# A decoder trunk's opening: modulation sums in four chunks of 256 columns, the first on TensorE

## The chip, the cores and the metric

The kernel runs on one core of a Trainium2 chip. The metric is the device time of one execution in microseconds. A profiled execution leaves a trace from which the rows below are read. Engines: TensorE (PE in the rows; PEld are its weight loads), VectorE (DVE), ScalarE (ACT), GpSimd (POOL) and SyncE (SP), which issues most of the DMA transfers. Each engine works through its own queue in a fixed order.

## What is computed

A trunk of two layers for one sequence of 256 tokens of width 1024, all in float32. Each layer is a feed-forward block, a mixer (attention in the first layer, a gated recurrence in the second) and another feed-forward block. Each block sees a normed x, scaled and shifted by modulations that come from a vector c. Only the first block matters here:

```python
cond = jax.nn.silu(c)
mod = (cond @ ada_w[i] + ada_b[i]).reshape(B, N_SUB, 3, 1, D)   # shift, scale, gate
h = rms_norm(x, norm_g[i, 0]) * (1.0 + mod[:, 0, 1]) + mod[:, 0, 0]
x = x + 0.5 * mod[:, 0, 2] * swiglu(h, ffn_w_up[i, 0], ffn_w_down[i, 0])
```

D is 1024, the feed-forward width 2816. `ada_w[i]` has 1024 rows and 9 x 1024 columns, `ffn_w_up` 1024 rows and 2 x 2816 columns.

## The kernel before

**Products.** Activations lie with their features on the partitions: `hbuf[k]` holds feature block k (128 of 1024) for all 256 tokens. Float32 products are made of three products of rounded halves (`mm3`, lines 728 to 730): high weight by high h, high weight by low h, low weight by high h. So each weight is split after it is loaded: ScalarE casts it to the rounded type (`wh`), VectorE takes the difference (`wl`). In the opening these are lines 360 and 361, later 371 and 372. Likewise h has a high half (line 588, ScalarE) and a low half (line 589, VectorE).

**Loads.** `plan` writes one list of items in the order in which they are loaded, `emit_raw` issues their transfers on the sync queue into a ring of eight raw buffers of 512 KB, `take_raw` hands them out in order. An item is split by `split_gen`, one step at a time. `pump` calls such a step at each tick, a tick being the three matmuls of one `mm3`, as long as it is no more than two weight items ahead (`SPLIT_AHEAD`).

**Side tasks.** `side` starts a generator that yields how many ticks it wants to wait; `tick` goes on with those that are due and `drain` finishes those that are named. A planner then fixes the order of each engine's queue: by program order, but past an instruction that by its own clock is not ready yet. `issue_after(i)` holds an instruction behind i on its engine.

**The opening** (`setup`). x is loaded, its squares are summed on ScalarE (556), the reciprocal root is taken on GpSimd (558), x is transposed on PE (614) and copied by ScalarE (616). VectorE scales x by the root (561) and the result is transposed and copied again, giving `xn`. Meanwhile the shift and scale columns of the first block come in eight chunks of 128 columns ("adc" items, 1 MB each), each followed by one "upk" item: the 128 rows of `ffn_w_up` that answer to it, for the first seven column blocks (`HEAD = 7`, 2 x 7 x 128 columns, 0.9 MB). In `ada_chunk` VectorE multiplies each of the 8 row blocks of an adc item by its value of `cond` and adds up, in two chains (434, 436); `NPE = 0` means that none of them is summed from raw weights on PE. `head_mods` lets PE add over the partitions, with the running sum as the stationary side and a column of ones (448); VectorE adds the bias and makes the scale (454, 457). Then ScalarE shifts and scales one feature block (585) and both halves of h are made (588, 589).

The loop over q in `setup` issues, for each chunk, first its modulations and its h, and then the products of the chunk before it (`cur`, `head_products`: 14 groups of three matmuls, 42). The seven column blocks are all open in PSUM at once, so the 336 matmuls of the opening can follow the order in which the weights come. Then `ffn` goes on with the column blocks from 7 on.

## Time and profile before

| | us |
|---|---|
| median of 3 runs | 1105.64 |
| lowest, highest | 1105.61, 1108.42 |
| the profiled execution | 1107.98 |
| its span | 1106.1 |
| PE busy in it | 1084.1 |
| VectorE, ScalarE busy | 838.7, 587.9 |
| transferred | 260.24 MB, 235 GB/s over the span |

The profiled execution is a fourth one; the rows are from it alone. In rows of the timeline the first number is the start in us from the beginning of the span, the second the time in us until the last instruction of the row has ended. The end of a matmul is modelled and matmuls overlap, so the distance of their starts tells more than their length. In brackets stands the idle time of the engine ahead of the row and what ended it.

### The profile page before, as it was taken

To read this page: it belongs to the slowest core of one execution; us is meant where nothing else is said; L and a number is where in the kernel's file an instruction comes from. 1 tells how busy PE (TensorE), PEld (TensorE's weight loads), DVE (VectorE), ACT (ScalarE), POOL (GpSimd) and SP (SyncE) were. 2 spreads that over 40 slices of the span, in tenths; PEclk is the share of its full clock that TensorE was granted. 3 is DMA by queue.
4 is the path that set the end of the run, shared out by engine and by line. 5 is a ranking of instruction groups with operands and counts; after the bars stand their busy time and mean duration, and the time that the engine had idled before them with its cause. 6 is when DMAs were issued, how large, how long until landed. Compare 5 with 4: busy or idle time off the path is not lost.

```text
span 1106.1 us, 22061 instructions
## 1 busy us (share of the span) xinstructions
PE 1084.1 (98%) x8835; PEld 1055.6 (95%) x8835; DVE 838.7 (76%) x1486; ACT 587.9 (53%) x1105; POOL 23.1 (2%) x46
## 2 busy tenths in 40 slices
PE   6999999999999999999999999999999999999997
PEld 6999999988999999999999999999998999999997
DVE  6987789587996797888579888777987879555542
ACT  5454444376865664444355444445777756444443
POOL 0000000020000000000000000000000000000000
PEclk9999999999999999999999999999999999999999
DMA  9999998759974579998958999995643456665530
GB/s 300 334 316 316 323 330 266 213 168 328 298 236 137 162 221 313 312 320 307 259 173 252 286 335 320 322 294 172 191 145 117 122 157 190 188 189 173 179 109 39
DMA packets 304707, 260.24 MB, mean 235 GB/s; under 512 B 9525, under 2 KB 281501, under 8 KB 304605
## 3 DMA queue, kind: packets, MB, share of 16 engines
q1 hardware_dynamic: 304172, 257.79, 76.0%
q8 instruction: 69, 1.13, 0.4%
q0 software_dynamic: 288, 0.52, 0.2%
q10 hardware_dynamic: 144, 0.52, 0.1%
q14 instruction: 34, 0.27, 0.1%
HBM read 257.75 MB, written 1.05 MB: 234 GB/s over the span
## 4 chain that ended last, share of the span: by engine, by line
PE 76%; issue 18%; ACT 3%; POOL 1%; DMA 1%; DVE 1%; SPq 0%; POOLq 0%; DVEq 0%; ACTq 0%
PE pf L729 17%; PE pf L728 16%; PE pf L730 16%; PE pd L728 6%; PE pd L729 6%; PE pd L730 6%; PE pA L1172 1%; ACT wh L371 1%; PE pv L881 1%; PE pv L879 1%; PE pv L880 1%; PE adaps L465 1%; PE sc L998 1%; DMA raw<-in_ffn_w_up_dram 1%; PE pt L1020 1%
## 5 line engine op out<-in xcount | busy, mean ns | idle before, releaser
L729 PE MATMUL pf<-hbuf,wh 128*128 128x256 f32 (+1 forms) x1920 | 543.8, 284 | 0.9 <-DVE hbuf L589 0.9
L730 PE MATMUL pf<-hbuf,wl 128*128 128x256 f32 (+1 forms) x1920 | 543.2, 284 | 0.0
L728 PE MATMUL pf<-hbuf,wh 128*128 128x256 f32 (+1 forms) x1920 | 539.0, 284 | 0.6 <-ACT hbuf L588 0.6
L371 ACT CAST wh<-raw 128x1024 fp32r<-128x1024 f32 x338 | 341.6, 1027 | 370.1 <-PE pf L729 219.0
L372 DVE TENSOR_TENSOR wl<-raw,wh 128x1024 fp32r<-128x1024 f32 x338 | 400.2, 1194 | 158.3 <-ACT wh L371 157.1
L728 PEld LDWEIGHTS pf<-hbuf,wh 128*128 128x128 f32 x1920 | 363.4, 191 | 4.8 <-issue 4.0
L729 PEld LDWEIGHTS pf<-hbuf,wh 128*128 128x128 f32 x1920 | 365.1, 190 | 1.2 <-DVE hbuf L589 1.1
L730 PEld LDWEIGHTS pf<-hbuf,wl 128*128 128x128 f32 x1920 | 364.6, 190 | 0.8 <-issue 0.8
L728 PE MATMUL pd<-gx,wh 128*128 128x256 f32 x704 | 197.5, 281 | 0.0
L729 PE MATMUL pd<-gx,wh 128*128 128x256 f32 x704 | 196.7, 279 | 0.0
L730 PE MATMUL pd<-gx,wl 128*128 128x256 f32 x704 | 196.4, 279 | 0.0
L412 DVE SCALAR_TENSOR_TENSOR adaacc<-raw,cond,adaacc 128x1024 f32<-128x1024 f32 x112 | 142.9, 1276 | 0.9 <-DMA raw<-in_ada_w_dram 0.4
L728 PEld LDWEIGHTS pd<-gx,wh 128*128 128x128 f32 x704 | 132.3, 188 | 2.5 <-issue 2.5
L730 PEld LDWEIGHTS pd<-gx,wl 128*128 128x128 f32 x704 | 132.3, 188 | 0.0
L729 PEld LDWEIGHTS pd<-gx,wh 128*128 128x128 f32 x704 | 132.3, 188 | 0.0
L794 ACT CAST gx<-g 128x256 fp32r<-128x256 f32 x88 | 35.6, 406 | 25.8 <-DVE g L836 18.3
L796 DVE TENSOR_TENSOR gx<-g,gx 128x256 fp32r<-128x256 f32 x88 | 36.6, 418 | 0.2
L410 DVE TENSOR_SCALAR adaacc<-raw,cond 128x1024 f32<-128x1024 f32 x16 | 12.1, 756 | 25.4 <-PE adaps L465 25.4
L836 DVE TENSOR_TENSOR g<-sa,pf 128x256 f32<-128x256 f32 x73 | 30.1, 414 | 0.4 <-ACT sa L835 0.2
L801 DVE SCALAR_TENSOR_TENSOR x<-pd,mod,x 128x256 f32<-128x256 f32 x32 | 14.3, 479 | 20.5 <-PE pd L730 20.5
L835 ACT ACTIVATE sa<-pf 128x256 f32<-128x256 f32 x73 | 27.4, 377 | 0.0
L360 ACT CAST wh<-raw 128x896 fp32r<-128x896 f32 x16 | 15.0, 935 | 23.0 <-DMA raw<-in_ffn_w_up_dram 23.0
(218 smaller groups left out, 859.2 us busy)
## 6 DMA issues: line engine op xcount, KB each, us to landing
raw<-in_ffn_w_up_dram SPq DMA_DIRECT2D x162, 512.0 KB, 5.5
raw<-in_ada_w_dram SPq DMA_DIRECT2D x128, 512.0 KB, 5.8
raw<-in_ffn_w_down_dram SPq DMA_DIRECT2D x76, 512.0 KB, 5.7
raw<-in_fox_w_in_dram SPq DMA_DIRECT2D x32, 512.0 KB, 5.3
raw<-in_hgrn_w_in_dram SPq DMA_DIRECT2D x32, 512.0 KB, 4.5
raw<-in_ada_w_dram SPq DMA_DIRECT2D x32, 256.0 KB, 6.9
raw<-in_ffn_w_up_dram SPq DMA_DIRECT2D x16, 448.0 KB, 6.6
raw<-in_fox_w_out_dram SPq DMA_DIRECT2D x8, 512.0 KB, 5.1
```

What stands on the lines that cost most here:

```text
L360: nc.scalar.copy(wh[:, k, cs], raw)
L371: nc.scalar.copy(wh[:, ks, cs], raw)
L372: nc.vector.tensor_tensor(wl[:, ks, cs], raw, wh[:, ks, cs].bitcast(F32), ALU.subtract)
L412: nc.vector.scalar_tensor_tensor(self.ada_acc, raw, self.cond[:, k:k + 1], self.ada_acc, ALU.mult, ALU.add)
L728: nc.tensor.matmul(ps, wh, hx[:, :n], start=first, stop=False, skip_group_check=True)
L729: nc.tensor.matmul(ps, wh, hx[:, lo:lo + n], start=False, stop=False, skip_group_check=True)
L730: nc.tensor.matmul(ps, wl, hx[:, :n], start=False, stop=last, skip_group_check=True)
L794: nc.scalar.copy(dst[:, :S], v)
L796: nc.vector.tensor_tensor(dst[:, lo:lo + S], v, dst[:, :S].bitcast(F32), ALU.subtract)
L801: nc.vector.scalar_tensor_tensor(self.x[:, m, :], ps, gate[:, m:m + 1], self.x[:, m, :], ALU.mult, ALU.add)
L835: nc.scalar.activation(sa, ps[0], AF.Silu)
L836: nc.vector.tensor_tensor(g, sa, ps[1], ALU.mult)
```

## The change

The chunks are twice as wide (`QA = 256`), so that there are four adc items of 2 MB, each followed by two upk items (`HEAD_ORDER`). The first adc item is not touched by VectorE: PE multiplies the raw weights, as the stationary side, by the columns of `cond`, 8 row blocks by 4 column groups, and adds up in PSUM. The other three are summed by VectorE in one chain of 512 elements, and then by PE over the partitions in four matmuls. What follows the sums is a side task (`head_task`) with lags of 4 ticks and 1 tick; the products of a feature block follow its own h. The bias and scale of a chunk are two VectorE instructions.

x is scaled on ScalarE by pairs of feature blocks, in place of VectorE, and the first copies of x are shared between ScalarE and VectorE. Four of the weight casts' instructions (second half of the first upk item, first half of the second, high and low) are held behind the latest shift. Six small loads go to GpSimd's queue. The transposes of the small rows share a bank.

The diff without the import and some of the removed lines, which the functions above show:

```diff
@@ -36,9 +36,9 @@
 FOLD = (5, 4)
 H_LAG = 0
 HEAD = 7
-QW = 128
-NPE = 0
-DEEP = 3
+QA = 256
+HEAD_LAG = (4, 1)
+HEAD_ORDER = [(0, 2), (2, 2), (4, 2), (6, 2)]
 HG_LAG = (4, 3, 4, 10, 12)
 FOX_LAG = (24, 6)
 HG_ORDER = [("hgq", 0), ("hgv", 0), ("hgq", 1), ("hgq", 2), ("hgv", 1), ("hgq", 3),
@@ -208,8 +208,8 @@
             extra = []
             if pos == 0:
                 assert kind == "ffn"
-                for q in range(D // QW):
-                    items += [("adc", (l, s, q)), ("upk", (f, q))]
+                for q, (k0, nk) in enumerate(HEAD_ORDER):
+                    items += [("adc", (l, s, q))] + [("upk", (f, k)) for k in range(k0, k0 + nk)]
                 extra = ada(n, (2,))
             take = quota.get(n, 0) if len(subs) == 6 else 24
             must = 0
@@ -253,12 +253,11 @@
             l, s, q = p
             c0 = s * 3 * D
             w = r(a["ada_w"][l])[:, :, c0:c0 + 2 * D].rearrange("p k (u f) -> p k u f", u=2)
-            return [(None, w[:, :, :, q * QW:(q + 1) * QW])], (KC, 2 * QW)
+            return [(None, w[:, :, :, q * QA:(q + 1) * QA])], (KC, 2 * QA)
         if kind == "upk":
             f, q = p
             w = r(a["ffn_w_up"][f // 2, f % 2]).rearrange("p k (u f) -> p k u f", u=2)
-            n = QW // P
-            return [(None, w[:, q * n:(q + 1) * n, :, 0:HEAD * P])], (n, 2 * HEAD * P)
+            return [(None, w[:, q:q + 1, :, 0:HEAD * P])], (1, 2 * HEAD * P)
         if kind == "up":
             f, j = p
             w = r(a["ffn_w_up"][f // 2, f % 2])
@@ -347,19 +346,15 @@
             self.ready[i] = (kind, wh, wl)
             return
         if kind == "upk":
-            wh, wl = [self.wp.tile([P, 2048], F32R, tag=t, name=f"{t}{i}")[:, :2 * HEAD * QW]
...
+            wh, wl = [self.wp.tile([P, 2048], F32R, tag=t, name=f"{t}{i}")[:, :2 * HEAD * P] for t in ("wh", "wl")]
+            for u in range(2):
+                cs = slice(u * HEAD * P, (u + 1) * HEAD * P)
+                raw = self.take_raw()
+                with self.tc.issue_after(self.last_shift[0]) if p[1] + u == 1 else nullcontext():
+                    nc.scalar.copy(wh[:, cs], raw)
+                with self.tc.issue_after(self.last_shift[1]) if p[1] + u == 1 else nullcontext():
+                    nc.vector.tensor_tensor(wl[:, cs], raw, wh[:, cs].bitcast(F32), ALU.subtract)
+                yield
             self.ready[i] = (kind, wh, wl)
             return
         t = self.wp.tile([P, 2048], F32R, tag="wh", name=f"wh{i}")
@@ -416,45 +411,58 @@
     def ada_chunk(self, p):
         nc = self.nc
         l, s, q = p
-        n = QW // P
...
+        n = 1024 // (2 * QA)
+        if q == 0:
+            ps = self.bank("adac")
+            for c in range(KC // n):
+                raw = self.take_raw()
+                for i in range(n):
+                    k = n * c + i
+                    for o in range(2 * QA // P):
+                        nc.tensor.matmul(ps[:, o:o + 1], raw[:, i, o * P:(o + 1) * P], self.cond[:, k:k + 1],
+                                         start=(k == 0 and o == 0), stop=(k == KC - 1), skip_group_check=True)
+                yield
+            self.side(("head", q), self.head_task(q, ps, self.xn), True)
+            return
+        ac = self.wk.tile([P, 2 * QA], F32, tag="mx", name=f"adc{q}", bufs=6)
+        for c in range(KC // n):
             raw = self.take_raw()
-            for i in range(m):
...
+            for i in range(n):
+                k = n * c + i
+                if k == 0:
+                    nc.vector.tensor_scalar(ac, raw[:, i, :], self.cond[:, k:k + 1], None, ALU.mult)
                 else:
-                    v = nc.vector.scalar_tensor_tensor(ac[:, k % 2], raw[:, i, :], self.cond[:, k:k + 1],
-                                                       ac[:, k % 2], ALU.mult, ALU.add)
+                    nc.vector.scalar_tensor_tensor(ac, raw[:, i, :], self.cond[:, k:k + 1], ac, ALU.mult, ALU.add)
             yield
-        self.head_acc[q] = (ac, ps)
...
+        self.side(("head", q), self.head_task(q, ac, self.xn), True)
+
+    def head_task(self, q, ac, xn):
+        nc = self.nc
+        l, s = divmod(self.subs[0], NSUB)
+        n = QA // P
+        if q == 0:
+            ps = ac
+        else:
+            ps = self.bank("adac")
             for o in range(2 * n):
-                nc.tensor.matmul(ps[:, o:o + 1], ac[:, j, o * P:(o + 1) * P], self.ones[:, 0:1],
...
+                nc.tensor.matmul(ps[:, o:o + 1], ac[:, o * P:(o + 1) * P], self.ones[:, 0:1],
+                                 start=(o == 0), stop=True, skip_group_check=True)
+        yield HEAD_LAG[0]
+        b = l * 72 + s * 24 + q * n
+        m = self.head_mod[:, :, q * n:(q + 1) * n]
+        nc.vector.tensor_tensor(m, ps[:, :2 * n].rearrange("p (u j) -> p u j", u=2),
+                                pick(self.adab[:, b:], [8, 2], [1, n]), ALU.add)
+        g = (l * 3 + s) * 8 + q * n
+        nc.vector.scalar_tensor_tensor(m[:, 1], m[:, 1], 1.0, self.vec[:, g:g + n], ALU.add, ALU.mult)
+        yield HEAD_LAG[1]
+        for k in range(q * n, (q + 1) * n):
+            u = self.w("u")
+            nc.scalar.activation(u, xn[:, k, :], AF.Identity, scale=self.head_mod[:, 1, k:k + 1],
+                                 bias=self.head_mod[:, 0, k:k + 1])
+            h = self.hbuf[0][:, k, :]
+            v0 = nc.scalar.copy(h[:, :S], u)
+            v1 = nc.vector.tensor_tensor(h[:, HS:HS + S], u, h[:, :S].bitcast(F32), ALU.subtract)
+            self.last_shift = (v0.ins, v1.ins)
 
     def ada_finish(self, l, s, part, total):
         nc = self.nc
@@ -521,12 +529,10 @@
                  (cst, a["consts"][:, P:])]
         for dst, src in small[:2]:
             nc.sync.dma_start(dst, src)
-        small = small[2:]
+        for dst, src in small[2:]:
+            nc.gpsimd.dma_start(dst, src)
         while len(self.raw_queue) < RAW_BUFS:
             self.emit_raw()
-            for dst, src in small[:2]:
-                nc.sync.dma_start(dst, src)
-            small = small[2:]
         self.ones = cp.tile([P, P], F32, name="ones")
         nc.vector.memset(self.ones, 1.0)
         self.sel4 = cst[:, 128:132]
@@ -550,50 +556,40 @@
         self.sq = None
         self.fold = None
         self.closing = False
-        self.head_acc = {}
+        self.xn = xn
         ms = self.wk.tile([P, 2], F32, tag="rstd", name="rstd")
         for t in range(2):
             nc.scalar.activation(xs[t], xt[t], AF.Square, accum_out=ms[:, t:t + 1])
         nc.vector.tensor_scalar(ms, ms, 1.0 / D, EPS, ALU.mult, ALU.add)
         self.last_pow = nc.gpsimd.tensor_tensor(ms, ms, self.mhalf, ALU.pow).ins
-        self.load_x(xt, self.x)
-        for t in range(2):
-            nc.vector.tensor_scalar(xs[t], xt[t], ms[:, t:t + 1], None, ALU.mult)
+        self.load_x(xt, self.x, engines=(nc.scalar.copy, nc.vector.tensor_copy))
+        self.split_step()
+        self.split_step()
+        self.vec = cp.tile([P, 80], F32, name="vec")
+        self.adab = cp.tile([P, 144], F32, name="adab")
+        self.head_mod = cp.tile([P, 2, KC], F32, name="headmod")
         pr = self.bank("pr")
-        nc.tensor.transpose(pr[:, :80], rows, self.ident[:80, :80])
-        self.vec = cp.tile([P, 80], F32, name="vec")
+        nc.tensor.transpose(pr[:, 0:80], rows, self.ident[:80, :80])
+        for l in range(2):
+            nc.tensor.transpose(pr[:, P + l * 72:P + (l + 1) * 72], abr[:, l, :], self.ident[:72, :72])
         nc.vector.tensor_copy(self.vec, pr[:, :80])
-        pa = self.bank("pa")
...
+        nc.vector.tensor_copy(self.adab, pr[:, P:P + 144])
+        for k in range(0, KC, 2):
+            for t in range(2):
+                c = slice(k * P, (k + 2) * P)
+                nc.scalar.activation(xs[t][:, c], xt[t][:, c], AF.Copy, scale=ms[:, t:t + 1])
+            self.load_x(xs, xn, k, k + 2)
+            if k in (0, 4):
+                self.split_step()
         self.pf = [self.acc("pf") for _ in range(3)] + [self.bank("pf") for _ in range(HEAD - 3)]
         self.pf = [self.halves(p) for p in self.pf]
-        l, s = divmod(self.subs[0], NSUB)
...
+        while self.n_split < 1:
+            self.split_step()
+        self.drain({("head", 0)})
+        for k in range(KC):
             wh, wl = self.weights("upk")
-            cur = [(q * n + i, wh[:, i], wl[:, i]) for i in range(n)]
-        for t in cur:
-            self.head_products(*t)
+            self.drain({("head", k * P // QA)})
+            self.head_products(k, wh, wl)
         with self.tc.issue_after(self.last_pow):
             for o in (0, 64):
                 nc.gpsimd.memset(self.bf[o:o + 64, :], 0.0)
@@ -606,14 +602,15 @@
             nc.vector.tensor_copy(self.identb, self.ident)
             nc.vector.tensor_copy(self.maskb, cst[:, 0:P])
 
-    def load_x(self, src, dst):
-        nc = self.nc
-        for k in range(0, KC, 2):
+    def load_x(self, src, dst, k0=0, k1=KC, engines=None):
+        nc = self.nc
+        engines = engines or (nc.scalar.copy,)
+        for k in range(k0, k1, 2):
             px = self.bank("px")
             for i in range(4):
                 nc.tensor.transpose(px[:, i * P:(i + 1) * P], src[i % 2][:, (k + i // 2) * P:(k + i // 2 + 1) * P],
                                     self.ident)
-            nc.scalar.copy(dst[:, k:k + 2, :].rearrange("p k c -> p (k c)"), px)
+            engines[k // 2 % len(engines)](dst[:, k:k + 2, :].rearrange("p k c -> p (k c)"), px)
 
     def head_products(self, k, wh, wl):
         for b in range(HEAD):
```

## Rows read from the trace of the kernel before

**Rows 1.** The profile's page: span, shares of the engines, one group of instructions.

```profile
span 1106.1 us, 22061 instructions
...
PE 1084.1 (98%) x8835; PEld 1055.6 (95%) x8835; DVE 838.7 (76%) x1486; ACT 587.9 (53%) x1105; POOL 23.1 (2%) x46
...
L412 DVE SCALAR_TENSOR_TENSOR adaacc<-raw,cond,adaacc 128x1024 f32<-128x1024 f32 x112 | 142.9, 1276 | 0.9 <-DMA raw<-in_ada_w_dram 0.4
```

**Rows 2.** Busy time by stretch: PE, PEld, DVE, ACT, POOL, granted clock, DMA share, GB/s.

```profile
0.00:5.00 5.00, 0.26 (x2) 0.20 (x2) 0.17 (x1) 1.70 (x4) 0.33 (x6) 1.00 0.53 171
5.00:10.00 5.00, 3.92 (x16) 3.11 (x16) 1.57 (x4) 4.47 (x8) 1.92 (x5) 1.00 1.12 309
10.00:15.00 5.00, 2.95 (x15) 2.98 (x16) 4.39 (x13) 2.39 (x4) 0.15 (x1) 1.00 1.09 333
...
21.14:27.07 5.93, 5.93 (x27) 5.93 (x28) 5.44 (x15) 2.57 (x4) 0.00 (x0) 1.00 1.12 334
...
61.06:65.30 4.24, 4.24 (x23) 4.24 (x24) 3.81 (x8) 1.42 (x3) 1.10 (x2) 0.60 1.10 324
...
80.00:200.00 120.00, 120.00 (x1023) 117.81 (x1023) 98.55 (x125) 53.37 (x81) 0.00 (x0) 1.00 1.00 309
```

**Rows 3.** Timeline of PE, 0 to 30 us: start, length, what was done.

```profile
6.38 2.82 PE L614 MATMUL px<-ident,startbig 128*128 128x128 f32 x12 [0.29 <-DMA startbig<-in_x_dram]
12.05 0.37 PE L563 MATMUL pr<-ident,startbig 80*128 80x80 f32 x1 [2.85 <-DMA cst<-in_consts_dram]
...
12.45 3.62 PE L614 MATMUL px<-ident,startbig 128*128 128x128 f32 x16
15.87 1.71 PE L448 MATMUL adac<-ones,adc 128*128 128x1 f32 x8
...
21.14 1.86 PE L728 MATMUL pf<-hbuf,wh 128*128 128x256 f32 x7 [0.56 <-ACT hbuf L588]
22.80 0.41 PE L729 MATMUL pf<-hbuf,wh 128*128 128x256 f32 x1
...
26.86 0.40 PE L730 MATMUL pf<-hbuf,wl 128*128 128x256 f32 x1
...
27.34 0.28 PE L728 MATMUL pf<-hbuf,wh 128*128 128x256 f32 x1
...
28.63 0.28 PE L729 MATMUL pf<-hbuf,wh 128*128 128x256 f32 x1
```

**Rows 4.** Timeline of PE, 56 to 72 us.

```profile
58.32 0.95 PE L448 MATMUL adac<-ones,adc 128*128 128x1 f32 x8
59.13 1.07 PE L728 MATMUL pf<-hbuf,wh 128*128 128x256 f32 x7
61.06 0.44 PE L729 MATMUL pf<-hbuf,wh 128*128 128x256 f32 x1 [0.86 <-DVE hbuf L589]
...
64.70 0.28 PE L728 MATMUL pf<-hbuf,wh 128*128 128x256 f32 x1
```

**Rows 5.** Groups by line and shape, 0 to 72 us: busy us, mean ns, idle before.

```profile
L729 PE MATMUL pf<-hbuf,wh 128*128 128x256 f32 x112 | 32.0, 300 | 0.9 <-DVE hbuf L589 0.9
...
L436 DVE SCALAR_TENSOR_TENSOR adc<-raw,cond,adc 128x256 f32<-128x256 f32 x48 | 19.7, 476 | 0.0
L361 DVE TENSOR_TENSOR wl<-raw,wh 128x896 fp32r<-128x896 f32 x16 | 17.5, 1091 | 3.7 <-ACT wh L360 3.6
L360 ACT CAST wh<-raw 128x896 fp32r<-128x896 f32 x16 | 15.0, 935 | 23.0 <-DMA raw<-in_ffn_w_up_dram 23.0
...
L600 POOL DMA_DIRECT2D bf<-in_fox_b_f_dram x2 | 1.2, 624 | 0.2 <-POOL bf L599 0.2
```

**Rows 6.** Timeline of VectorE, 0 to 90 us.

```profile
59.31 0.22 DVE L454 TENSOR_TENSOR headmod<-adac,adab 128x1 f32<-128x1 f32 x2 [2.06 <-PE adac L448]
```

**Rows 7.** Timeline of ScalarE, 0 to 90 us.

```profile
59.69 0.60 ACT L585 ACTIVATE u<-startbig,headmod 128x256 f32<-128x256 f32 x1 [1.69 <-DVE headmod L457]
...
61.13 0.40 ACT L588 CAST hbuf<-u 128x256 fp32r<-128x256 f32 x1
```

More of the change, by code (lines that the diff above doesn't have):

```diff
@@ L1 @@
 import math
-from contextlib import ExitStack
+from contextlib import ExitStack, nullcontext
 import numpy as np
@@ L418, in ada_chunk @@
         l, s, q = p
-        n = QW // P
-        ac = self.wk.tile([P, 512], F32, tag="mx", name=f"adc{q}", bufs=6).rearrange("p (j c) -> p j c", j=2)
-        ps = self.bank("adac")
-        first = True
-        m = 512 // QW
-        for c in range(KC // m):
-            raw = self.take_raw()
-            for i in range(m):
-                k = m * c + i
-                if k < NPE:
-                    for o in range(2 * n):
-                        nc.tensor.matmul(ps[:, o:o + 1], raw[:, i, o * P:(o + 1) * P], self.cond[:, k:k + 1],
-                                         start=first, stop=False, skip_group_check=True)
-                        first = False
-                elif k < NPE + 2:
-                    nc.vector.tensor_scalar(ac[:, k % 2], raw[:, i, :], self.cond[:, k:k + 1], None, ALU.mult)
-                else:
-                    v = nc.vector.scalar_tensor_tensor(ac[:, k % 2], raw[:, i, :], self.cond[:, k:k + 1],
-                                                       ac[:, k % 2], ALU.mult, ALU.add)
+        n = 1024 // (2 * QA)
@@ L440, in ada_chunk @@
-        self.last_chain = v.ins
-    def head_mods(self, l, s, q):
+        self.side(("head", q), self.head_task(q, ac, self.xn), True)
+    def head_task(self, q, ac, xn):
         nc = self.nc
-        n = QW // P
-        ac, ps = self.head_acc.pop(q)
-        for j in range(2):
-            for o in range(2 * n):
-                nc.tensor.matmul(ps[:, o:o + 1], ac[:, j, o * P:(o + 1) * P], self.ones[:, 0:1],
-                                 start=(NPE == 0 and o == 0 and j == 0), stop=(j == 1), skip_group_check=True)
-        for part in (1, 0):
-            b = l * 72 + (s * 3 + part) * 8 + q * n
-            m = self.head_mod[:, part, q * n:(q + 1) * n]
-            with self.tc.issue_after(self.last_chain):
-                nc.vector.tensor_tensor(m, ps[:, part * n:(part + 1) * n], self.adab[:, b:b + n], ALU.add)
-            if part == 1:
-                g = (l * 3 + s) * 8 + q * n
-                nc.vector.scalar_tensor_tensor(m, m, 1.0, self.vec[:, g:g + n], ALU.add, ALU.mult)
+        l, s = divmod(self.subs[0], NSUB)
[4 more added lines that the diff above has]
+            ps = self.bank("adac")
+            for o in range(2 * n):
+                nc.tensor.matmul(ps[:, o:o + 1], ac[:, o * P:(o + 1) * P], self.ones[:, 0:1],
[16 more added lines that the diff above has]
+            self.last_shift = (v0.ins, v1.ins)
@@ L562, in setup @@
         pr = self.bank("pr")
-        nc.tensor.transpose(pr[:, :80], rows, self.ident[:80, :80])
-        self.vec = cp.tile([P, 80], F32, name="vec")
+        nc.tensor.transpose(pr[:, 0:80], rows, self.ident[:80, :80])
+        for l in range(2):
+            nc.tensor.transpose(pr[:, P + l * 72:P + (l + 1) * 72], abr[:, l, :], self.ident[:72, :72])
         nc.vector.tensor_copy(self.vec, pr[:, :80])
-        pa = self.bank("pa")
-        for l in range(2):
-            nc.tensor.transpose(pa[:, l * 72:(l + 1) * 72], abr[:, l, :], self.ident[:72, :72])
@@ L593, in setup @@
+        self.drain({("head", 0)})
+        for k in range(KC):
             wh, wl = self.weights("upk")
-            cur = [(q * n + i, wh[:, i], wl[:, i]) for i in range(n)]
-        for t in cur:
-            self.head_products(*t)
+            self.drain({("head", k * P // QA)})
+            self.head_products(k, wh, wl)
         with self.tc.issue_after(self.last_pow):
```

30 lines of the change are left out of this document (removed).

## The prediction

> **What bounds the kernel now.** Read the shares first: TensorE (PE) is busy for 98% of the span [rows 1]. Then the stretches: behind the opening it has no idle time left (120.00 of 120.00 us between 80 and 200 us) [rows 2]. Whatever moves the end of the opening therefore moves the end of the kernel, one for one, unless the weights then come too late. So I read the opening, in order of time, engine by engine.
>
> On PE [rows 3] it goes: 16 transposes of x (to 9.20 us), three small ones, 16 transposes of the normed x, two groups of sums of the modulations, and at 21.14 us the first product. The 336 products of the first seven column blocks run from there to about 71.9 us: the table of groups that ends at 72 us holds 112 of each of the three kinds [rows 5]. Inside these 50.7 us stand four costs that are not products at full speed:
> - The low clock at the start. From 22.80 to 26.86 us 19 products take 0.214 us each; from 27.34 to 28.63 us 11 take 0.117 [rows 3]. 256 columns in 0.214 us are 1.2 per ns: the 1.2 GHz level, though the granted-clock column shows 1.00 there [rows 2], presumably because nothing had yet changed that it could record. About 27 products ran so: 27 x 0.097 = 2.6 us lost.
> - Six groups of sums between products, 0.81 us each (58.32 to 59.13) [rows 4]: 4.9 us.
> - A pause of 0.86 us ahead of 61.06 us [rows 4]. VectorE waits 2.06 us for the last group of sums, with the low half of the current chunk of h queued behind [rows 6]; PE waits for that half.
> - The low clock again after that pause: 17 products from 61.06 to 64.70 us [rows 4], granted clock 0.60 in the stretch [rows 2]: 17 x 0.097 = 1.6 us.
>
> The remaining 336 x 0.1175 = 39.5 us are products, and some 1.3 us is unevenness. The DMA is also nearly full in the opening (309 to 334 GB/s) [rows 2], but PE does not wait for it once products run.
>
> **The change part by part.**
>
> *The first chunk on PE.* Four sums of 256 columns replace eight of 128. For the first, each of the 8 row blocks times 4 column groups is one matmul with raw weights as the stationary side. One such fp32 matmul is two in the trace (the four calls of a group appear as 8) [rows 3], so the first chunk is 64. Eight took 1.71 us at 15.87 us, 0.21 each [rows 3]: 64 x 0.21 = 13.4 us. At the higher clock a group of eight took 0.81, so 64 would be 6.5. That is the fork of this case. I take 0.21, because PE worked without a break from 12.05 to 17.58 us on transposes and sums, and the products that followed still ran at the low level [rows 3].
>
> The Trainium skill (TensorE: Matmul & The Clock Gate, section LDWEIGHTS) prices a weight load at its columns over 1.2 GHz, 107 ns for 128. By that 64 loads would be an estimated 6.8 us and the first product would come some 6.6 us sooner than in my sum. The row says 0.21 us for each at the low clock, so the measurement decides.
>
> *When the first product starts.* By the window rows 0.86 MB have moved at 5 us, 2.40 at 10, 4.07 at 15 [rows 2]. x, identity, small constants and the first 2.10 MB chunk are 3.4 MB, so that chunk is there at 13.0 us and the first weights (0.92 MB more) at about 15.8; its first quarter is there before PE has finished the x transposes at 9.20. So PE, not the DMA, sets the start: 9.2 + 13.4 + 0.4 (three small transposes) + 2.7 (12 of the 16 transposes of the normed x, 3.62 us for 16) = 25.7 us. The last four are queued behind the last sum and lie beside what follows it: modulation 0.38 us (59.31 to 59.69), shift 0.60, cast 0.40 [rows 6, 7], 1.4 us together. With some latency that is 27.3 us; 28.2 if all 16 transposes stand ahead, 26.5 if eight stand behind. Against 21.14 this is +6.2 us (bounds +5.4 to +7.1).
>
> *What it gives back.* Sums inside the products: three groups of eight instead of six, -2.4 us. The products of a chunk follow its own shift now, and the modulation of the next chunk is queued 4 ticks (12 products, 1.4 us) behind its sums, so VectorE no longer stands waiting ahead of the current h: the pause of 0.86 and the 1.6 us of low clock behind it go. Next late there would be the weights. The 17.0 MB up to the last of them are there at about 53.5 us if the DMA goes on at 0.333 MB/us from 5 us [rows 2]; the last chunk's products begin near 67 us, so there is room. The ramp at the first product stays as it is, about 2.6 us (bounds 1.6 to 2.7, as the clock rose 3.5 us or 5.9 us after work began in the two cases seen) [rows 3, 4].
>
> *VectorE.* It loses the first chunk (two chains of 8 steps, 0.476 us each). A 512-element step lies between 0.476 us (256) and 1.276 us (1024) [rows 1, 5], by their line 0.74; eight are 5.9 us per two weight chunks, where two chains of 256 were 7.6. Nothing on the path: its data wait for PE in the new opening.
>
> *Scaling on ScalarE.* Eight instructions at 0.60 us [rows 7], 4.8 us, between the x copies (two of the four go to VectorE) and about 16 us, when PE first wants them after the two first quarters of the sum (9.2 + 6.7). Hidden by PE's sums; were these half as long, some 2 us of it would show.
>
> *The small loads.* Six transfers leave the sync queue and go to GpSimd's. The two of that queue took 0.62 us each [rows 5]; six are 3.7 us from 0.9 us on, over before the reciprocal root that shares that engine, which needs the squares of all of x, the last of it used by PE from 6.38 us [rows 3]. They feed the three small transposes, wanted at about 16 us. The sync queue issues the first chunk without them; PE is later than either. Zero; bounds -0.3 and +1 us if they crowd x.
>
> *Two casts held behind a shift* (second half of the first weights, first half of the second). ScalarE's 0.94 us per half [rows 5] come after the shift of chunk 1. At 0.214 us the 14 products that need only the high parts last 3 us, which covers the held half.
>
> **The sum.** +6.2 - 2.4 - 0.9 - 1.6 = +1.3 us on the profiled execution, 1107.98 us (span 1106.1 and 1.9 around it): 1109.3. That execution is 2.3 us above the median of the three runs, 1105.64. The pause with its low clock, 2.5 us, is the one thing in the opening that can come and go by so much, so what I count as saved may not be in the median run. I take half of the difference off: **1108.0 us, 2.4 above the median**, own range 1105.5 to 1110.5. A run of this kernel can tell about 0.3% from no change: under 1102.3 is faster, over 1109.0 slower.
>
> **Rivals.**
>
> *The sums themselves raise the clock.* For: PE has never yet run 6.7 us of nothing but these matmuls; the transposes and the sums of the unbroken stretch at 12 to 17.6 us need not count alike. Against: that stretch. If they count, the rise comes 3.5 us (61.06 to 64.70) to 5.9 us (21.14 to 27.07) after 9.2 us. Then 17 to 28 of the 64 are done; the rest go at 0.10 us, 4.7 to 3.6; with 1.7 to 3.1 of transposes the sums end at 19.1 to 21.8 and products start at 20.5 to 23.2, say 21.7, at once at full speed. Sum: +0.6 - 2.4 - 0.9 - 1.6 - 2.6 = -6.9, on the same footing 1099.9; I say 1100.5, between 1098 and 1103, since the weights behind the opening would be wanted 7 us sooner and the DMA (309 GB/s between 80 and 200 us against 334 earlier) has few per cent to spare [rows 2]. The Trainium skill (TensorE: Matmul & The Clock Gate, Part 1) speaks for this: sustained matmul activity releases the clock. The trace agrees for products; for sums like these no row shows it either way.
>
> *A later rise.* The clock rises only near the end of the sums, as the products start: -2.6 and a little, 1104.
>
> *Slower: the weights' first cast queued behind both shifts.* ScalarE's order is fixed ahead. If the first half's cast stands behind the shifts of chunks 0 and 1, the first product waits 1.0 + 0.94 us more [rows 5, 7]: 1110. It decides where the planner thought the sums of the first chunk quick, so that its shift was ready before these weights.
>
> *Slower: PE stands at the second chunk's sums.* They are placed by ticks among the first products; behind them all products wait. A VectorE chain of 5.9 us that starts only after the first modulation, four weight splits ahead of it (4 x 1.09 us) [rows 5], ends some 11 us after 26 us; the first two chunks' products last until about 40. Only a place in the first chunk's products makes a wait, of about 3 us: 1111.
>
> *The change does nothing*: not likely, as the start itself moves.
>
> **How the numbers follow.** Forecast 0.46 (seven tenths of it within 0.3%, the rest slower); sums raise the clock 0.25 (faster); later rise 0.08 (within); cast behind the shifts 0.16 (slower); PE at the second sums 0.05 (slower). Faster 0.25, same 0.32 + 0.08 = 0.40, slower 0.14 + 0.16 + 0.05 = 0.35. Range 1099 to 1111: it reaches into the raised clock as far as 1099 and leaves out the rest of it, the stall and the upper edge, under 0.2.
>
> **What would show it.** In the changed kernel: 64 matmuls on adac from raw, at 0.21 or at 0.10 us; the first product at 27 us or at 21; the spacing of its first thirty products; three groups of eight sums later; no idle time on PE near 60 us and no low clock there; the 112th product of each kind at about 73 us. Wrong if the spacing of the sums falls to 0.10 midway, or if products wait for a weight cast.

## The result and the profile after

The changed kernel takes 1112.74 us, the median of six runs (1112.09 to 1113.87); the kernel before took 1105.79 beside it. The ratio is 1.006 (95% interval 1.0048 to 1.0072): slower by 6.95 us. The forecast was 1108.0, with 1111 as the upper end of its range.

The page of the profile after, its span and the engines' shares (the profiled execution itself took 1112.09 us):

```profile
span 1110.3 us, 22077 instructions
...
PE 1086.9 (98%) x8859; PEld 1058.6 (95%) x8859; DVE 830.4 (75%) x1430; ACT 589.5 (53%) x1111; POOL 26.6 (2%) x52
```

PE is busy for 2.8 us longer than in [rows 1] and the span is 4.2 us longer. The end of the opening is found by the groups of instructions up to 77.5 us (busy time, mean ns, idle time ahead), and by the timelines of PE, the kernel before and then the kernel after:

```profile
L727 PE MATMUL pf<-hbuf,wl 128*128 128x256 f32 x112 | 31.9, 293 | 0.0
```

```profile
71.76 0.28 PE L730 MATMUL pf<-hbuf,wl 128*128 128x256 f32 x1
...
228.32 1.06 PE L688 MATMUL rb<-diag,ones 128*128 128x128 f32 x4 [1.19 <-DVE diag L687]
```

```profile
77.41 0.28 PE L727 MATMUL pf<-hbuf,wl 128*128 128x256 f32 x1
...
233.97 0.75 PE L685 MATMUL rb<-diag,ones 128*128 128x128 f32 x4 [1.19 <-DVE diag L684]
```

The 112th product with low weights starts at 77.41 us, in the kernel before at 71.76. So the opening became 5.65 us longer. At the end of a pause of 1.19 us that both kernels have, at 228.32 and 233.97 us, the two are still 5.65 us apart; the span has grown by only 4.2. The 1.4 us between them go together with a low clock behind that pause, which the profiled execution of before had and that of after did not (stretches, before and then after; columns as in [rows 2]: length; busy time of PE, PEld, DVE, ACT, POOL; granted clock; DMA share; GB/s):

```profile
228.00:232.00 4.00, 3.68 (x18) 3.71 (x19) 2.70 (x8) 2.51 (x6) 1.92 (x7) 0.57 0.16 62
```

```profile
234.00:238.00 4.00, 4.00 (x33) 4.00 (x34) 3.01 (x9) 3.17 (x8) 1.62 (x6) 1.00 0.01 4
```

At 0.57 of the clock, 4.00 us lose an estimated 1.7. This stands far behind the opening, and other variants of the wide kernel have it too (the clock falls at 232.5 us in the first experiment below), so it is not the change. It is also the nearest thing on record to a reason why the profiled execution of before was 2.2 us above its own median.

The timeline of PE, kernel after, 0 to 40 us (start, length, work, in brackets the idle time ahead of it and what ended it):

```profile
7.15 2.78 PE L611 MATMUL px<-ident,startbig 128*128 128x128 f32 x12 [0.53 <-DMA startbig<-in_x_dram]
9.77 0.50 PE L422 MATMUL adac<-cond,raw 128*128 128x1 f32 x4
...
10.23 1.44 PE L422 MATMUL adac<-cond,raw 128*128 128x1 f32 x12
...
14.80 2.56 PE L422 MATMUL adac<-cond,raw 128*128 128x1 f32 x12
...
19.49 2.56 PE L422 MATMUL adac<-cond,raw 128*128 128x1 f32 x12
...
26.29 0.58 PE L725 MATMUL pf<-hbuf,wh 128*128 128x256 f32 x1 [2.42 <-ACT wh L354]
...
30.08 0.36 PE L727 MATMUL pf<-hbuf,wl 128*128 128x256 f32 x1
30.28 0.28 PE L725 MATMUL pf<-hbuf,wh 128*128 128x256 f32 x1
...
37.63 1.84 PE L448 MATMUL adac<-ones,adc 128*128 128x1 f32 x8 [3.66 <-DVE adc L435]
```

The stretches of the opening, kernel after:

```profile
10.00:15.00 5.00, 5.00 (x41) 5.00 (x40) 1.19 (x4) 1.71 (x4) 1.56 (x5) 0.82 1.08 374
15.00:20.00 5.00, 5.00 (x28) 5.00 (x26) 0.00 (x0) 1.25 (x3) 0.00 (x0) 0.50 1.06 374
20.00:25.00 5.00, 3.86 (x18) 3.46 (x18) 0.38 (x3) 3.48 (x9) 0.00 (x0) 0.50 0.69 205
25.00:30.00 5.00, 3.71 (x17) 3.72 (x18) 4.10 (x6) 4.06 (x6) 0.00 (x0) 0.50 0.39 115
...
40.00:45.00 5.00, 5.00 (x30) 5.00 (x30) 3.34 (x6) 3.25 (x6) 0.00 (x0) 0.61 0.77 254
...
55.00:60.00 5.00, 5.00 (x44) 5.00 (x44) 4.82 (x9) 2.62 (x5) 0.00 (x0) 1.00 1.03 397
```

What the two views show, in order:
- **The sums.** All 64 raw matmuls are there, from 9.77 to 22.05 us. The first start every 0.11 us (12 between 10.23 and 11.53), those from 14.80 on every 0.21 (12 in 2.56). The granted clock falls in the middle of them: 0.82 in the stretch 10 to 15 us, 0.50 in the next, with PE busy for 5.00 of 5.00 us in both.
- **The first product** starts at 26.29 us, 5.15 later than in [rows 3]; PE stands 2.42 us ahead of it, waiting for the first weight cast.
- **The ramp.** At 30.08 us products still come every 0.21 us, from 30.28 on every 0.117. That makes some 18 slow ones, 27 before.
- **A pause of 3.66 us** (33.97 to 37.63) at the sums of the second chunk, which wait for VectorE's chain. They stand behind the 48th of the 84 products of the first chunk, and the other 36 stand behind them.
- **The clock** is low again after that pause (0.61 from 40 to 45 us); the eight sums take 1.84 us instead of 0.81, and some 21 products 0.097 more each.
- **At 60 us** PE has no idle time and a granted clock of 1.00; the pause and the low clock of [rows 4] are gone.

The account against before: start +5.15, pause +3.66, sums at the low clock +1.0, products at the low clock behind the pause +2.0; less three groups of sums (-2.4), the pause at 60 us with its low clock (-2.5) and the shorter first ramp (-0.8). That is +6.1; the end of the opening moved by 5.65.

Where the pause comes from stands in the timeline of VectorE, kernel after:

```profile
22.09 0.16 DVE L453 TENSOR_TENSOR headmod<-adac,adab 128x4 f32<-128x4 f32 x1 [9.66 <-PE adac L422]
...
24.94 0.43 DVE L464 TENSOR_TENSOR hbuf<-u,hbuf 128x256 fp32r<-128x256 f32 x1 [2.49 <-ACT hbuf L463]
26.26 1.09 DVE L356 TENSOR_TENSOR wl<-raw,wh 128x896 fp32r<-128x896 f32 x1 [0.90 <-ACT wh L354]
...
27.61 3.09 DVE L356 TENSOR_TENSOR wl<-raw,wh 128x896 fp32r<-128x896 f32 x3
30.62 0.48 DVE L433 TENSOR_SCALAR adc<-raw,cond 128x512 f32<-128x512 f32 x1
31.13 4.69 DVE L435 SCALAR_TENSOR_TENSOR adc<-raw,cond,adc 128x512 f32<-128x512 f32 x6
...
36.74 0.74 DVE L435 SCALAR_TENSOR_TENSOR adc<-raw,cond,adc 128x512 f32<-128x512 f32 x1
```

VectorE stands 9.66 us, until the raw sums give it the first modulation. Then it waits twice for ScalarE (2.49 and 0.90 us), and from 26.26 on it works without a pause until the chain ends at 37.4 us: one low half of h (the other came at 24.94), five splits of 1.0 to 1.1 us, and the chain, whose eight steps of 512 elements take 0.48 and seven times 0.74 to 0.78. Four of the splits stand ahead of the chain, one ahead of its last step. From the modulation to the end of the chain it takes 15.0 us, 3.4 of them waits for ScalarE.

And where the 2.42 us ahead of the first product come from, in the timeline of ScalarE, kernel after:

```profile
23.05 0.58 ACT L613 COPY startbig<-px 128x512 f32<-128x512 f32 x1 [1.52 <-PE px L611]
23.53 0.60 ACT L460 ACTIVATE u<-startbig,headmod 128x256 f32<-128x256 f32 x1
24.03 0.57 ACT L613 COPY startbig<-px 128x512 f32<-128x512 f32 x1
24.50 0.41 ACT L463 CAST hbuf<-u 128x256 fp32r<-128x256 f32 x1
24.80 0.60 ACT L460 ACTIVATE u<-startbig,headmod 128x256 f32<-128x256 f32 x1
25.30 0.93 ACT L354 CAST wh<-raw 128x896 fp32r<-128x896 f32 x1
```

Between the first modulation (22.45) and the first weight cast (25.30) stand two copies that need the last eight transposes (which PE does behind the sums), two shifts and one cast of h.

### The profile page after: what moved, and what is told of

The parts are those of the page before. It is cut to its first block, busy times and chain, and to the rows that moved or that the text cites. A ratio compares the mean times of both kernels' runs of the same rounds, so it can differ in the third digit from the quotient of the medians.

```text
span 1110.3 us, 22077 instructions
## 1 busy us (share of the span) xinstructions
PE 1086.9 (98%) x8859; PEld 1058.6 (95%) x8859; DVE 830.4 (75%) x1430; ACT 589.5 (53%) x1111; POOL 26.6 (2%) x52
## 4 chain that ended last, share of the span: by engine, by line
PE 76%; issue 18%; ACT 2%; DVE 1%; POOL 1%; DMA 1%; SPq 0%; POOLq 0%; DVEq 0%; ACTq 0%
PE pf L725 16%; PE pf L726 16%; PE pf L727 16%; PE pd L725 6%; PE pd L726 5%; PE pd L727 5%; PE pA L1169 1%; PE pv L878 1%; PE pv L877 1%; PE pv L876 1%; ACT wh L366 1%; PE adac L422 1%; PE adaps L473 1%; PE sc L995 1%; PE pt L1017 1%
## 5 line engine op out<-in xcount | busy, mean ns | idle before, releaser
L876 PE MATMUL pv<-wh,hbuf 128*128 128x512 f32 x64 | 26.0, 406 | 0.0
```

Of the source, the lines that this page charges most:

```text
L876: nc.tensor.matmul(pss[t], hh, wh[:, i, :], start=(k == 0), stop=False)
```

## The experiments

**The first chunk by VectorE.** Everything else of the change stays.

```diff
-        if q == 0:
+        if False:
```
(in `ada_chunk` and in `head_task`)

> The first chunk is summed by VectorE like the other three; nothing else differs from the changed kernel. Theory S (the 64 raw matmuls at 0.21 us are the loss: they set the first product and, through the modulations that wait for them, everything queued on VectorE): the chunk's last quarter is there at about 13.5 us, VectorE needs 1.5 us for it, the group of eight 1.7, modulation and shift 1.4, a weight cast ahead of PE 0.9: first product at 18 to 20 us instead of 26.3, pause before the second chunk's sums under 1 us, total 1103 to 1106. Rival L (the small loads on GpSimd's queue, x later by 0.8 us and its scaling on ScalarE are the loss): first product not before 23 us, total above 1110.

Measured: 1111.84 us, ratio 1.0041 (1.0026 to 1.0056). Timeline of PE:

```profile
9.38 0.37 PE L572 MATMUL pr<-ident,startbig 80*128 80x80 f32 x1 [2.86 <-DMA startbig<-in_final_norm_g_dram]
...
9.79 2.76 PE L611 MATMUL px<-ident,startbig 128*128 128x128 f32 x12
...
24.43 0.58 PE L725 MATMUL pf<-hbuf,wh 128*128 128x256 f32 x1 [2.51 <-ACT wh L354]
...
35.77 1.84 PE L448 MATMUL adac<-ones,adc 128*128 128x1 f32 x8 [3.92 <-DVE adc L435]
```

The first product comes 1.9 us sooner, not 6 to 8, and the total is over 1110, as rival L had it: at 9.38 us PE has waited 2.86 us for the last of the small loads, now on GpSimd's queue, with 12 transposes of x queued behind the small ones. And the pause at the second chunk's sums is still there, 3.92 us. So the raw sums on PE cannot be the whole loss, and the small loads cost something once PE's opening is short.

**Four more buffers for the first chunk.** Does the ring of eight raw buffers hold the second chunk's transfers back? The first chunk's four raws go to unused stretches of the tile `big`, so that the ring holds only later items (the counts of the ring in `setup` and `take_raw`, not shown here, leave them out too).

```diff
-        t = self.rawp.tile([P, 1024], F32, tag="raw", ...)
+        if i == 0:
+            o = (6144, 7808, 8832, 9856)[half]
+            t = self.big[:, o:o + 1024]
+        else:
+            t = self.rawp.tile([P, 1024], F32, tag="raw", ...)
```

> The changed kernel, with the first chunk loaded into four unused stretches of the startup buffer instead of the ring, so that its slow sums hold no ring buffer and the transfers behind it go on. Theory R (the ring is held, the second chunk's loads come late, so PE waits at its sums): DMA between 20 and 30 us rises from 115 to 205 GB/s to over 300, the pause of 3.66 us falls under 1 us, total 1108 to 1109. Theory Q (VectorE's queue: the second chunk's chain stands behind the first chunk's modulation, h and weight splits, whenever its data come): DMA the same rise, but the chain starts at about 30 us as before and the pause stays at 3 to 4 us, total 1112 to 1113.

Measured: 1115.48 us, ratio 1.0074 (1.0057 to 1.0091). Timeline of PE, then the stretches:

```profile
9.38 0.85 PE L426 MATMUL adac<-cond,startbig 128*128 128x1 f32 x4
...
22.19 2.56 PE L426 MATMUL adac<-cond,startbig 128*128 128x1 f32 x12
...
28.98 0.58 PE L730 MATMUL pf<-hbuf,wh 128*128 128x256 f32 x1 [2.42 <-ACT wh L358]
...
40.33 1.02 PE L452 MATMUL adac<-ones,adc 128*128 128x1 f32 x8 [2.91 <-DVE adc L439]
```

```profile
20.00:25.00 5.00, 5.00 (x26) 5.00 (x26) 0.18 (x2) 2.78 (x6) 0.00 (x0) 1.00 0.68 214
25.00:30.00 5.00, 2.58 (x12) 2.18 (x11) 1.61 (x4) 4.26 (x9) 0.00 (x0) 1.00 0.00 0
```

Both theories expected the DMA to speed up between 20 and 30 us; it slows to 214 GB/s and then to nothing. The eight ring buffers then hold two weight chunks and the second chunk, and nothing empties them while VectorE and ScalarE stand behind the first modulation. The pause is still 2.91 us. VectorE's chain starts without waiting for data and ends 15.0 us after the modulation, as in the changed kernel, so the ring is not the cause. This execution also had the sums at 0.21 us from the first one on, and its first product came at 28.98.

**Both at once** (no new edit).

> Both: first chunk summed by VectorE, and loaded outside the ring. If S holds and the ring is no limit once VectorE sums, the same as the run with VectorE alone within 1 us; if the ring still limits (R), 1 to 2 us faster than that.

Measured: 1111.06 us, ratio 1.0036 (1.0023 to 1.0049); first product at 24.10, pause 2.95 us. It lies within 1 us of the run without the buffers: the ring limits neither variant.

**The later chunks' sums 14 ticks further back.**

```diff
+            if q:
+                yield 14
```
(ahead of the sums in `head_task`)

> The changed kernel, with 14 more ticks (42 products) ahead of each later chunk's sums on PE. Theory Q: products that were queued behind the sums run first, the pause at 34 us goes or moves 33 products (3.9 us) on, where the chain is done; a shorter pause of 1 to 2.5 us for modulation and shift comes ahead of the third weight chunk; total 1109.5 to 1111. Rival (the chain sets the third chunk's h anyway, so the order of PE does not matter): pause of the same 3 to 4 us in another place, total 1112 to 1113.

Measured: 1113.57 us, ratio 1.0054 (1.0037 to 1.0072). Timeline of PE:

```profile
41.68 0.95 PE L450 MATMUL adac<-ones,adc 128*128 128x1 f32 x8
45.38 1.01 PE L727 MATMUL pf<-hbuf,wh 128*128 128x256 f32 x3 [2.75 <-ACT hbuf L465]
```

The total is not theory Q's; it lies 0.6 us above its rival's range. No pause at the sums now, but 2.75 us at 45.38, where products need the h that follows from them. In this execution too all raw sums ran at 0.21 us (first product at 29.02), which may hide part of the effect. Its mean of the granted-clock column is 0.996 (the column reads 1.00 until its first change, so a late rise makes the mean higher; see the last section), and the three of the five executions with that mean took 1113.6 to 1114.6 us; the other two, with 0.987 and 0.988, took 1110.8 and 1111.0. The changed kernel's six divide in the same way: two with 0.996 took 1113.9, four with 0.987 took 1112.1 to 1112.9 (its trace is one of the four). So where the raw sums begin at the high clock, the later place may be worth 1 to 2 us; no trace shows such an execution. What is shown is that most of the loss stays: the pause comes back at the next instruction that needs VectorE.

**Another order of loads**: the second chunk ahead of the second weights.

```diff
-HEAD_ORDER = [(0, 2), (2, 2), (4, 2), (6, 2)]
+HEAD_ORDER = [(0, 1), (1, 2), (3, 2), (5, 3)]
```

> The changed kernel with one weight chunk between the first and the second modulation chunk instead of two (loads: modulations 0, weights 0, modulations 1, weights 1 and 2, ...). Theory Q (the second chunk's chain stands on VectorE behind the splits of two weight chunks): it now stands behind one, starts 2.2 us sooner, and the pause of 3.66 us falls to 1 to 2 us; with less low clock behind it, total 1109 to 1111. Rival D (the data of the second chunk come late, as the ring is held): they are loaded before weights 1, so the pause goes altogether and the wait is for weights 1 instead; total as the changed kernel, 1112 to 1113.

Measured: 1112.65 us, ratio 1.0069 (1.0049 to 1.0089). Timeline of PE, the row with the largest pause:

```profile
33.81 0.63 PE L727 MATMUL pf<-hbuf,wl 128*128 128x256 f32 x2 [2.45 <-DVE wl L356]
```

The chain is early, and now the split of the second weights is late: 2.45 us of waiting in another place and the same total. In these two orders the sum of what VectorE has to do behind the first modulation counts, not which part comes first.

**Small loads back on the sync queue**, first chunk by VectorE.

```diff
-        for dst, src in small[2:]:
-            nc.gpsimd.dma_start(dst, src)
+        small = small[2:]
         while len(self.raw_queue) < RAW_BUFS:
             self.emit_raw()
+            for dst, src in small[:2]:
+                nc.sync.dma_start(dst, src)
+            small = small[2:]
```

> The run with the first chunk on VectorE (e1_dve0), and the small loads back on the sync queue between the raw loads as in the kernel before. There PE waited 2.86 us for the last small load with 12 transposes of x behind, and VectorE began the first chain at 13.2 us. Rival L (the small loads on GpSimd's queue cost the start): PE's wait before the small transposes goes, the chain begins at 10 to 11 us, first product at 21 to 22 us instead of 24.4, total 1108 to 1109.5. If the start is set by ScalarE's order (shift, copy, cast ahead of the first product): first product unchanged at 24 us and total 1111 to 1112.

Measured: 1107.48 us, ratio 1.0013 (1.0003 to 1.0023); first product at 21.81, pauses of 1.63 and 0.87 us, end of the opening at 70.5. Against the first experiment that is 3.1 us for the queue of six small loads; with it, the small transposes now stand behind the transposes of x on PE and no longer ahead of them.

**The same with the other order of loads** (the edits of the last two).

> Wide chunks with the three suspected costs of the opening taken away together: first chunk on VectorE, small loads on the sync queue, one weight chunk between the first two modulation chunks. If start and pause add up as separate causes: first product at 21 to 22 us, pause under 2 us, total 1105.5 to 1108. If taking away the start's delay only lengthens the pause (theory Q: VectorE's work from the first shift to the second chunk's end is what counts): pause 3 to 5 us and total 1108.5 to 1110.5.

Measured: 1108.17 us, ratio 1.0016 (1.0005 to 1.0027); first product at 22.08, pause 2.75 us at 29.69. Again the order changes nothing that the intervals resolve.

**Chunks of 128 columns.** The changed kernel with chunks as narrow as before; the first is still summed on PE, now in 32 matmuls.

```diff
-QA = 256
+QA = 128
-HEAD_ORDER = [(0, 2), (2, 2), (4, 2), (6, 2)]
+HEAD_ORDER = [(k, 1) for k in range(8)]
```

> The changed kernel with chunks of 128 columns again, one weight chunk behind each; the first still summed on PE (32 matmuls instead of 64), everything else as changed. Theory W (the width: a second chunk needs 2 MB, 5.9 us of VectorE and all of its two shifts in one piece, before its first product): first product at 19.5 to 21 us, no pause over 1.5 us after it, total 1105 to 1107, about the kernel before. Rival (the parts around it, the queued sums and the small loads, carry the loss): total 1110 or more.

Measured: 1104.68 us, ratio 0.9996 (0.9984 to 1.0009); first product at 20.90, behind it one pause over 1 us (1.18 us at 53.25), end of the opening at 70.0. The whole loss is gone with the width. Three things go with it: VectorE's chain is half as long, the modulation comes sooner (the 32 raw sums end at 13.7 us), and the chain starts ahead of the splits (at 15.3 us, with one split within it where there were four ahead). This run does not part them.

**Width by who sums.** Four kernels with the side parts undone alike: small loads on the sync queue, and x scaled by VectorE:

```diff
-                nc.scalar.activation(xs[t][:, c], xt[t][:, c], AF.Copy, scale=ms[:, t:t + 1])
+                nc.vector.tensor_scalar(xs[t][:, c], xt[t][:, c], ms[:, t:t + 1], None, ALU.mult)
```

> The changed kernel with two side parts undone: small loads back on the sync queue, x scaled by VectorE. Theory S (the 64 sums on PE set the start, so what is ready earlier waits for them): x is ready about 1 us sooner, first product 25 to 27 us if the sums begin at the high clock, 28 to 29 if not, total 1110.5 to 1113. Rival L (these side parts carry part of the loss here too): first product by 3 us or more sooner, total under 1109.

> e7_dve0_sp (wide chunks, first on VectorE, small loads on the sync queue) with x scaled by VectorE instead of ScalarE. There 1107.5, first product at 21.8 us, pauses of 1.6 and 0.9 us ahead of the second and third sums. If ScalarE's scaling and its order hold the first product: 20 to 20.5 us, total 1106 to 1107. If VectorE, which now has 8 x 0.25 us more ahead of the first chain, sets it: 22.5 us or later, 1107.5 to 1109.

> Chunks of 128 columns (as e8_q128, 1104.7), first on PE, with small loads on the sync queue and x scaled by VectorE; what is left of the change is the first chunk on PE, the queued sums and modulations and the shared copies. In e8 the first product (20.9 us) waited for the chain of x: scaling, transposes, copies on ScalarE. With x 0.7 us sooner and its scaling off ScalarE: first product at 18.5 to 20 us, no pause over 1 us, total 1102 to 1104.5, faster than the kernel before. If DMA or VectorE then sets the pace: pauses among the later chunks and 1104.5 to 1106.

> As e10_q128_sp_dvex, but the first chunk on VectorE too: of the change only the queued sums with their merged modulations and the shared copies are left. Against e10 it tells what the sum on PE is worth at 128 columns: VectorE has 3 us more ahead of its other work and PE 32 matmuls less. If PE's sums are cheap there (half as many, PE would wait for x anyway): e10 0.5 to 2 us faster than this. If they cost as at 256: this 1 to 3 us faster than e10.

| ratio to before (95%) | chunks of 256 | chunks of 128 |
|---|---|---|
| first chunk on PE | 1.0061 (1.0041 to 1.0082), 1113.63 us | 0.9994 (0.9981 to 1.0008), 1106.17 us |
| first chunk by VectorE | 1.0004 (0.9993 to 1.0015), 1107.40 us | 0.9971 (0.9959 to 0.9983), 1103.22 us |

A ratio of 0.001 is 1.1 us. Against before the four are +6.7, -0.7, +0.4 and -3.2 us. What is left of the change in the last one (sums queued among products, a chunk's bias and scale in two instructions, shared copies of x and the smaller parts) is together worth 3.2 us of gain. From there width alone costs 3.6, summing on PE alone 2.5, both 9.9. Their 3.8 on top of the sum is hardly more than what the four intervals leave uncertain together (some 3.3 us).

Against what was expected: the first has its product at 26.55, within 25 to 29, and is 0.6 us above the range of its total. The second starts at 22.21 and takes 1107.40, between its two cases. The third lies 0.2 us above the case in which DMA or VectorE sets the pace. The fourth is 2.5 us faster than the third by the ratios: the sums on PE cost there too.

The first of the four also shows no cost of the side parts in the changed kernel (1.0061 against 1.0060, with intervals of 0.002 and 0.001 either way). For the VectorE variant the scaling comes to 1.0 us, which the intervals don't resolve.

The changed kernel with the side parts undone, timeline of PE:

```profile
26.55 0.58 PE L727 MATMUL pf<-hbuf,wh 128*128 128x256 f32 x1 [3.08 <-ACT wh L354]
...
36.69 1.02 PE L448 MATMUL adac<-ones,adc 128*128 128x1 f32 x8 [1.43 <-DVE adc L435]
```

The narrow kernel with PE's sums starts its products at 18.34 but stands 3.70 us at 25.04, at the next chunk's sums: expected were 1102 to 1104.5, so the early start is worth nothing here. In its timeline of VectorE the chain stands behind the first modulation (15.09) and then waits for its data as well:

```profile
17.19 0.35 DVE L433 TENSOR_SCALAR adc<-raw,cond 128x256 f32<-128x256 f32 x1 [1.75 <-DMA raw<-in_ada_w_dram]
```

Three splits stand between its steps, and it ends at 24.9. So in this variant the loads have a share in the pause. The narrow kernel with VectorE's sums, timelines of PE and of VectorE:

```profile
19.41 1.01 PE L727 MATMUL pf<-hbuf,wh 128*128 128x256 f32 x3 [1.85 <-ACT hbuf L463]
...
23.47 0.85 PE L448 MATMUL adac<-ones,adc 128*128 128x1 f32 x4
...
30.15 0.58 PE L448 MATMUL adac<-ones,adc 128*128 128x1 f32 x4
```

```profile
16.42 0.35 DVE L433 TENSOR_SCALAR adc<-raw,cond 128x256 f32<-128x256 f32 x1
16.80 0.48 DVE L435 SCALAR_TENSOR_TENSOR adc<-raw,cond,adc 128x256 f32<-128x256 f32 x1
17.60 0.16 DVE L453 TENSOR_TENSOR headmod<-adac,adab 128x2 f32<-128x2 f32 x1 [0.31 <-PE adac L448]
```

Its chain for the next chunk begins (16.42, 16.80) before the modulation of the present one (17.60), and PE doesn't wait at the sums at 23.47 and 30.15. It is the fastest kernel here; its interval against the kernel before, 0.9959 to 0.9983, leaves out 1.

Not tried: the chain of the wide second chunk ahead of the first modulation in VectorE's queue while PE sums. That would be the direct test of the reading that VectorE's order is the cause; it rests so far on the traces, on the width, and on the ring and the order of loads having changed nothing. A larger ring was not tried either.

## Why the prediction was wrong

The step that failed is the one on VectorE: **"Nothing on the path: its data wait for PE in the new opening."** The data were not what it waited for. Its queue stood behind the first modulation, 9.66 us, and only then came the low halves of h, the splits and the chain, 15.0 us in all. The right end of that chain stood in the rivals: "some 11 us after 26 us", 37 us; it measured 37.4. What made it harmless there was "the first two chunks' products last until about 40". That compares the chain with the time when PE runs out of products, while PE works in order and meets the sums after 48 of 84, at 33.97. The pause was given 3 us (3.66 measured) and 1111, but a chance of 0.05, and the low clock behind it was not counted: 1.0 us in the sums and 2.0 in the products. Together that is 6.7 us, more than the 4.35 by which the opening misses the sum of +1.3. Neither of the two other arrangements tried, the sums further back on PE and the second chunk loaded earlier, took the loss away.

The other steps:
- **Start at 27.3 us**: 26.3, and 29.0 in two runs with the low clock from the first sum. Near, but by luck, as errors cancel: the 64 sums took 10.1 us instead of 13.4, since about half of them ran at the high level (from 9.77 to 21.91 us it is 12.1, less 1.8 for eight transposes of the normed x and 0.3 for the small ones); eight transposes and not four came behind them, and from the last sum to the first product it took 4.4 us, not 1.6. The rival in which the cast stands behind both shifts was true in its order: both come ahead of the first cast, which starts 2.85 us after the modulation, and PE waits 2.42 us for it.
- **"The sums themselves raise the clock"**, at 0.25 the largest rival: false. The clock fell during them and rose 3.9 us after products began. It had risen at about 9.8 us, when only transposes had run.
- **Three groups of sums, no idle time and no low clock at 60 us**: right (5.00 of 5.00 us, clock 1.00). The reading of the pause in the kernel before leaves out that a weight split (1.09 us from 59.58 on) stood between VectorE's modulation and the low half of h.
- **The ramp at the first product**: 1.8 us, within its bounds of 1.6 to 2.7.
- **Scaling on ScalarE, small loads**: no cost seen in the changed kernel, as put. The small loads cost 3.1 us where PE's opening is short; "PE is later than either" was the cover, and it held only with the raw sums on PE.
- **The DMA**: right, neither transfers nor ring buffers held up the first product or the second chunk's sums in the changed kernel.
- **The two casts held behind a shift**: no run takes the holds out, so what they do is not shown.
- **Half of the 2.3 us by which the profiled run of before lay above its median** taken off: the medians differ by 6.95 us, the two profiled runs by 4.1. The prediction gave the pause at 60 us as the reason; the trace has a likelier one that the change does not touch, the low clock at 228 to 232 us (an estimated 1.7 us). Then the +1.3 belongs on the median as it stands, which gives 1106.9, further from the result: this term hid part of the miss. With one trace of before it stays open.

## What to carry to other kernels

When work moves to another engine, list what stands in each other engine's queue behind its result, and add up that queue from the moment the result comes; compare its end with the time at which the in-order consumer meets it, not with the time at which the consumer runs out of ready work. A chunk's width is the grain of such a pipeline: with the first chunk summed on PE, 128 columns cost nothing against the kernel before (-0.7 us, not resolved) and 256 cost 6.7 us; against VectorE's sums at the same width it is 2.5 and 6.3. A pause in TensorE can be paid twice: behind the 3.66 us the products ran at the low clock and lost 2.0 us more. It need not be: behind the 1.63 us in the run with the small loads back on the sync queue the clock stayed at 1.00.

## What was not expected of the hardware

In the changed kernel TensorE was busy for 5.00 of 5.00 us with the sums, matmuls with raw float32 weights and a single moving column, and the granted clock fell from the 2.4 GHz level to the 1.2 GHz level in their midst, at about 13.2 us. It stayed there for 17 us and rose at 30.2 us, after 3.9 us of products of 256 columns. In the run with four more buffers sums and transposes filled TensorE from 9.38 us to the last transposes at 26.6, and their spacing was 0.21 us throughout: the clock did not rise. The Trainium skill (TensorE: Matmul & The Clock Gate, Part 1) says that sustained matmul activity releases the clock. The trace agrees for the products; in these runs the sums neither kept the clock up nor raised it.

The clock at the first sums differs between executions. In the changed kernel the last transposes of x ahead of them come every 0.21 us (12 from 7.15 to 9.77) and the sums from 9.77 on every 0.11: the clock rose between the two. In two of its variants the first sums, at 9.4 us, came every 0.21 as the transposes did, and the first product followed at 29.0 instead of 26.3; what decides between the two is not shown. (A transpose shows the two levels as well: in the narrow kernel with PE's sums they come every 0.213 us up to 16.0 and every 0.11 from 16.2 on.) The granted-clock column reads 1.00 at the low level too: 1.00 from 20 to 25 us in the run with four more buffers, where 12 sums from 22.19 on took 2.56 us. So at the opening the spacing of the matmuls tells the level, not the column.
